# One core, a hybrid pooling and attention layer: its first stage (token scaling, q/k/v projections, q/k chains) with the weight bounds, the rotation, the transposes and the opening remade

## The chip, the cores and the metric

The kernel runs on one core of one Trainium2 chip. The metric is the device time of one execution in microseconds (us); the time before is the median of three runs. Smaller is better. The five engines are named as the profile names them: PE (TensorE), DVE (VectorE), ACT (ScalarE), POOL (GpSimd), SP (SyncE, which here only issues DMAs).

## What is computed

One layer over 2048 latent tokens and 256 context tokens of 1024 channels. The part that matters here is the front of it:

```python
h = _rmsnorm(x, norm_g) * (1.0 + scale[:, None, :]) + shift[:, None, :]
hc = _rmsnorm(xc, norm_g) * (1.0 + scale_c) + shift_c
p = _split_proj(h @ w_in)
...
def prep(t, nh, g):
    t = _rmsnorm(t.reshape(b, n, nh, -1), g)
    return t if tables is None else _rope_2d(t, tables)
...
def _rotate(x, cos, sin):
    m = x.shape[-1] // 2
    x1, x2 = x[..., :m], x[..., m:]
    return jnp.concatenate([x1 * cos - x2 * sin, x1 * sin + x2 * cos], axis=-1)
```

Each 64-wide head of q and k is normalised and rotated, its first 32 channels by the token's row in the grid and its last 32 by the column. Differential attention, grouped-query attention, pooling, gates and the two output projections follow. Scores are sums over the 64 channels, so an order of channels within a head that is the same for q and k changes nothing.

## The kernel before

All products run in split half precision: a float32 matrix is scaled by a power of two, written as a high and a low float16 part, and three products (high·high, high·low, low·high) are summed. The power of two comes from a bound on the largest absolute value.

There are three stages, one after the other. The first ends near 640 us, the second (attention, with gate columns computed between) and third (merge) take the rest; the diff does not touch those two.

The first stage, in order:

1. **Opening.** The two modulation vectors (`ada_product`, 16 weight blocks of 512 KB), then `modulation`, then `token_scale`, which bounds the modulated tokens over all partitions: a PE transpose to one row, a DVE maximum, and a PE product with a row of ones (`onerow`) that spreads it. `hfirst` and `hscaled` make the first 384 tokens (256 context, 128 latent) into float16 pairs. `w_prepare("dv")` bounds and splits the first weights.
2. **Five projections** in the order `QKV_ORDER` = dv, dk, dq, gq, gkv, called kinds below. The loop goes over tiles of 128 tokens: 18 tiles for dv, dk and gkv, 16 for dq and gq. `project` issues 24 products of 512 columns for a tile (256 columns for gkv) into one of three PSUM buffers `acc`, and then moves every open `qk_chain` one step.
3. **The q/k chain of a tile** is a generator with three steps, one step per later tile. Step one: squares on ACT (`sq`), their sums on DVE (`s`), and on POOL the power -1/2 (`r`, line 350) and the two products that join gain and rotation tables (`ab`). Step two: DVE normalises (`nt`), POOL multiplies by the cosine part (`rt`, line 362), DVE makes the sine part in two products (`m`, line 367), and DVE adds both (line 371). Step three: four PE transposes (`tpq`), ACT's high half and DVE's low half (`sp`, lines 378 and 379), stores by SP.
4. **Beside the products**, `beside` steps other generators in the middle of a tile: `w_prepare` of the next kind (line 436: a DVE maximum for each of 8 weight tiles; then `all_max`, a POOL reduction over partitions at line 420; then the split into halves, ACT and DVE), and `scan`, which reads the 40 gate columns (512 KB each) and takes a DVE maximum of each (line 471), and then `all_max` too. In gq, `ada_product` for the residual gate runs between the tiles.

Every engine executes its instructions in the order in which the code emits them, and SP issues DMAs in that order too, so an instruction that waits holds up all that stands behind it on its engine.

Of the kernel before, what the change touches and what calls it, by code (L numbers as in the profile page):

```python
# [35 lines left out]
HTOP = 8192.0  # L36
TINY = 2.0 ** -30
# [19 lines left out]
def block_kernel(ctx: ExitStack, tc, x, xT, ctxt, cc, ada_w, ada_bT, norm_gT, w_qkv, w_gate, gains,  # L57
# [149 lines left out]
    with tc.tile_pool(name="p1", bufs=1) as sp, tc.tile_pool(name="p1s", bufs=1, space=PSUM) as pp:  # L207
# [71 lines left out]
        def turned_tokens(g, k, gain, shift):  # L279

            nctx = max(0, min(3, NCT - 3 * g)) * P
            tp = tpx("tpx")
            for i in range(3):
                nc.tensor.transpose(out=tp[:, i * P:(i + 1) * P], in_=xs[g][i][:, k * P:(k + 1) * P], identity=ident)
            hf = sp.tile([P, GT], F32, name="hf", tag="hf", bufs=5)
            for a, b, m in ((0, nctx, 1), (nctx, GT, 0)):
                if b > a:
                    nc.scalar.activation(out=hf[:, a:b], in_=tp[:, a:b], func=AF.Identity, scale=gain[:, k, m:m + 1],
                                         bias=shift[:, k, m:m + 1])
            return hf  # L290

        def hfirst():

            for k in range(KT):
                hf0.append(turned_tokens(0, k, gainT, shiftT))
                yield

        def hscaled():
            for k in range(KT):
                hT[k] = s8("hT", [P, 2, SEQ], F16)  # L300
                for a, b, d in targets(0, k, 0):
                    nc.scalar.activation(out=d, in_=hf0[k][:, a:b], func=AF.Copy, scale=hsc[:, 0:1])
                for (a, b, d), (_, _, h) in zip(targets(0, k, 1), targets(0, k, 0)):
                    nc.vector.scalar_tensor_tensor(out=d, in0=hf0[k][:, a:b], scalar=hsc[:, 0:1], in1=h, op0=ALU.mult,
                                                   op1=ALU.subtract)
                yield
# [10 lines left out]
        def token_scale():  # L317
# [8 lines left out]
            row = tpx("hbt")  # L326
            nc.tensor.transpose(out=row[0:1, 0:P], in_=hb[:, 0:1], identity=ident)
            m1 = sp.tile([1, 1], F32, name="m1")
            nc.vector.tensor_reduce(out=m1, in_=row[0:1, 0:P], axis=AX.X, op=ALU.max)
            every = tpx("hbb")  # L330
            nc.tensor.matmul(every[:, 0:1], lhsT=onerow, rhs=m1, start=True, stop=True)
            nc.vector.tensor_scalar(out=hb[:, 1:2], in0=every[:, 0:1], scalar1=TINY, scalar2=None, op0=ALU.max)
# [6 lines left out]
        def qk_chain(ps, nh, gi, t, eps, dst):  # L339
# [11 lines left out]
            if t >= NCT:  # L351

                ab = sp.tile([P, 2, 64], F32, name="ab", tag="ab", bufs=3)
                nc.gpsimd.tensor_tensor(out=ab[:, :, 0:32], in0=rrow[:, t - NCT], in1=g4[:, gi, :, 0:32], op=ALU.mult)
                nc.gpsimd.tensor_tensor(out=ab[:, :, 32:64], in0=rcol, in1=g4[:, gi, :, 32:64], op=ALU.mult)
# [4 lines left out]
            rt = sp.tile([P, 512], F32, name="rt", tag="rt", bufs=2)  # L360
# [52 lines left out]
        def all_max(mx, name):  # L413

            m = sp.tile([P, 1], F32, name=name, tag="amx", bufs=2)
            nc.vector.tensor_reduce(out=m, in_=mx, axis=AX.X, op=ALU.max)
            nc.vector.tensor_scalar(out=m, in0=m, scalar1=TINY, scalar2=None, op0=ALU.max)
            r = sp.tile([P, 1], F32, name=name, tag="amr", bufs=2)
            from concourse import bass_isa
            nc.gpsimd.partition_all_reduce(out_ap=r, in_ap=m, channels=P, reduce_op=bass_isa.ReduceOp.max)  # L420
            return r
# [9 lines left out]
        def w_prepare(kind):  # L431

            width = QKV_CHUNKS[kind][1]
            mx = sp.tile([P, KT], F32, name="wmx", tag="wmx", bufs=2)
            for k in range(KT):
                nc.vector.tensor_reduce(out=mx[:, k:k + 1], in_=wraws[kind][k][:, :width], axis=AX.X, op=ALU.max,
                                        apply_absolute_value=True)
                yield
            r = all_max(mx, "wm")
            yield  # L440
            do, undo = scale_of(sp, HTOP, r, "ws")
            yield
            weights[kind] = []
            for k in range(KT):
                wr = wraws[kind][k]
                wt = sp.tile([P, 2, 512], F16, name="wt", tag="wt", bufs=16)
                nc.scalar.activation(out=wt[:, 0, :width], in_=wr[:, :width], func=AF.Copy, scale=do[:, 0:1])
# [14 lines left out]
        def scan():  # L462

            tiles = []
            for i in range(41):
# [4 lines left out]
                if i:  # L470
                    nc.vector.tensor_reduce(out=gmx[:, i - 1:i], in_=tiles[i - 1], axis=AX.X, op=ALU.max,
                                            apply_absolute_value=True)
                yield
            r = all_max(gmx, "gm")
            yield
            do, undo = scale_of(sp, HTOP, r, "gs")
# [9 lines left out]
        def project(kind, width, wt, t):  # L486
# [102 lines left out]
        for n, (half, k) in enumerate(blocks):  # L589
# [7 lines left out]
            if n == 8:  # L597
                modulation(0, ada_turn(rws))
            if n in (10, 11, 12, 13):
                next(hm)  # L600
        rws = ada_rows(aps[1])
        modulation(1, ada_turn(rws))
        hsc, hundo = token_scale()
        for _ in range(KT + 2):
            next(wp)
        hs = hscaled()
        for k in range(4):
            next(hs)
        for k in range(4):
            next(hm)  # L610
            next(hs)
            next(wp, None)
        for s in (hm, hs, wp):
            for _ in s:
                pass
        for _ in xnorm(1):
            pass
        scanning = scan()
        for n, kind in enumerate(QKV_ORDER):
# [12 lines left out]
            for t in range(first, NT):  # L632
# [8 lines left out]
                if n == 0:  # L641
# [8 lines left out]
                    if u >= 2:  # L650
                        at_step(coming, 4, *((7,) if u >= 12 else ()))
# [21 lines left out]
                if final:  # L673
                    if u < 2:
                        for _ in range(2):
                            next(scanning, None)
                    if u == 3:
                        for _ in scanning:
                            pass
                    if u in (4, 5):  # L680
                        col_load(u - 4)
                    if u == 9:
# [547 lines left out]
def make_inputs(i):  # L1230
# [13 lines left out]
    o["w_qkv"] = np.concatenate([sl(1536, 2048), sl(2048, 2560), sl(3584, 3840), sl(1024, 1536), sl(3072, 3584)], axis=1)  # L1244
# [3 lines left out]
    o["gains"] = np.stack([g, g.reshape(4, 2, 2, 16)[:, :, ::-1].reshape(4, 64)], axis=1)[None]  # L1248
# [43 lines left out]
```

## Time and profile before

| what | value |
|---|---|
| median of 3 runs | 3000.75 us (2998.82 to 3003.14) |
| the profiled execution's own time | 2999.54 us |
| its span | 2997.8 us |
| PE, DVE, ACT, POOL busy | 2800.9, 2322.5, 1569.1, 706.5 us |
| first stage: first qkv product to the end of gkv's | 54.8 to 632.9 us |

The span is the time from the first to the last profiled instruction; the time of the execution is 1.7 us longer. Busy times of different engines overlap. A row of a timeline gives start, length, engine, line, operation and tiles, and in brackets the idle time of the engine before the row and what ended it. A row of the table of stretches gives the stretch, its length, the busy time (and count) of the products of one line and of their weight loads, the granted clock, the DMA share and GB/s.

### The profile page before, as it was taken

To read this page: it belongs to the slowest core of one execution; us is meant where nothing else is said; L and a number is where in the kernel's file an instruction comes from. 1 tells how busy PE (TensorE), PEld (TensorE's weight loads), DVE (VectorE), ACT (ScalarE), POOL (GpSimd) and SP (SyncE) were. 2 spreads that over 40 slices of the span, in tenths; PEclk is the share of its full clock that TensorE was granted. 3 is DMA by queue.
4 is the path that set the end of the run, shared out by engine and by line. 5 is a ranking of instruction groups with operands and counts; after the bars stand their busy time and mean duration, and the time that the engine had idled before them with its cause. 6 is when DMAs were issued, how large, how long until landed. Compare 5 with 4: busy or idle time off the path is not lost. (4 is left out here: it accounts for less than half of the span.)

```text
span 2997.8 us, 40968 instructions
## 1 busy us (share of the span) xinstructions
PE 2800.9 (93%) x15013; PEld 1650.1 (55%) x15013; DVE 2322.5 (77%) x2953; ACT 1569.1 (52%) x2040; POOL 706.5 (24%) x689
## 2 busy tenths in 40 slices
PE   6997978889999999999999999999999997999999
PEld 1543433545555555555555556555565554787787
DVE  3557975649888889888889888889888875756753
ACT  3731111226766666666776777766777662223221
POOL 0024543540110111211112111111201114433431
PEclk8999989989999999999999999999999998999999
DMA  6233543238888888789899898899997986677674
GB/s 244 106 113 96 152 119 97 56 78 181 182 164 175 174 179 174 157 180 177 180 187 201 177 186 173 172 194 190 186 185 159 188 164 209 228 247 247 205 254 154
DMA packets 1134265, 516.45 MB, mean 172 GB/s; under 512 B 985040, under 2 KB 1038704, under 8 KB 1134064
## 3 DMA queue, kind: packets, MB, share of 16 engines
q1 hardware_dynamic: 1134064, 513.84, 72.9%
q8 instruction: 118, 1.93, 0.3%
q14 instruction: 83, 0.68, 0.1%
HBM read 208.24 MB, written 78.97 MB: 96 GB/s over the span
## 5 line engine op out<-in xcount | busy, mean ns | idle before, releaser
L177 PE MATMUL gate<-hT,gws 128*128 128x512 f16 x3840 | 871.7, 381 | 0.0
L177 PEld LDWEIGHTS <-gws 128*128 128x128 f16 x3840 | 374.1, 98 | 421.1 <-issue 21.0
L771 ACT ACTIVATE pt<-sa,nm,escale 128x1024 f32<-128x1024 f32 x256 | 308.3, 1204 | 451.9 <-DVE nm L768 400.8
L763 PEld LDWEIGHTS <-qt 128*128 128x128 f16 x2560 | 250.4, 98 | 354.4 <-issue 71.6
L491 PE MATMUL qkv<-wt,hT 128*128 128x512 f16 (+1 forms) x1920 | 399.8, 364 | 0.0
L767 DVE TENSOR_REDUCE nm<-sb 128x1 f32<-128x1280 f32 x256 | 379.1, 1481 | 0.5 <-PE sb L763 0.4
L766 DVE TENSOR_REDUCE nm<-sa 128x1 f32<-128x1024 f32 x256 | 311.2, 1216 | 72.1 <-PE sa L763 63.0
L772 ACT ACTIVATE pt<-sb,nm,escale 128x1280 f32<-128x1280 f32 x256 | 360.4, 1408 | 0.0
L854 DVE SCALAR_TENSOR_TENSOR lo<-pt,nm,hi 128x2304 f16<-128x2304 f32 x128 | 339.7, 2654 | 5.5 <-ACT hi L849 4.7
L763 PE MATMUL sb<-kt,qt 128*128 128x512 f16 (+1 forms) x1536 | 320.5, 345 | 18.5 <-ACT pt L772 17.5
L849 ACT ACTIVATE hi<-pt,nm 128x2304 f16<-128x2304 f32 x128 | 283.3, 2213 | 92.9 <-issue 49.3
L491 PEld LDWEIGHTS <-hT 128*128 128x128 f16 x1920 | 191.4, 100 | 182.6 <-issue 17.9
L763 PE MATMUL sa<-kt,qt 128*128 128x512 f16 x1024 | 263.4, 380 | 21.6 <-ACT pt L771 21.2
L1141 PE MATMUL br<-bt,wt 128*128 128x512 f32 x1152 | 268.7, 394 | 2.5 <-DVE wt L996 2.5
L894 PE MATMUL av<-th,vt 128*128 128x256 f16 x2304 | 262.6, 273 | 8.2 <-DMA th<-hi 5.4
L1141 PEld LDWEIGHTS br<-bt,wt 128*128 128x128 f32 x1152 | 217.7, 189 | 52.2 <-DVE wt L996 3.6
L894 PEld LDWEIGHTS <-vt 128*128 128x128 f16 x2304 | 225.1, 98 | 36.2 <-issue 6.0
L878 POOL TENSOR_TENSOR o<-ot 128x256 f32<-128x256 f32 x32 | 22.0, 687 | 841.5 <-ACT ot L874 799.4
L162 POOL TENSOR_SCALAR gws<-gw 128x512 f16<-128x512 f32 x74 | 75.6, 1022 | 604.1 <-PE gate L177 600.3
L378 ACT ACTIVATE sp<-tpq 128x512 f16<-128x512 f32 (+1 forms) x68 | 34.8, 512 | 318.0 <-PE tpq L376 315.4
L868 PE MATMUL av<-th,vt 128*128 128x256 f16 x1728 | 198.9, 273 | 0.0
L1173 PE MATMUL out<-y,wt 128*128 128x512 f32 x768 | 183.5, 397 | 12.0 <-DVE wt L996 5.3
(195 smaller groups left out, 3321.1 us busy)
## 6 DMA issues: line engine op xcount, KB each, us to landing
tD<-gt SPq DMA_DIRECT2D x96, 256.0 KB
wr<-in_w_br SPq DMA_DIRECT2D x32, 768.0 KB
ld<-tD SPq DMA_DIRECT2D x96, 256.0 KB
scan<-in_w_gate SPq DMA_DIRECT2D x40, 512.0 KB
gw<-in_w_gate SPq DMA_DIRECT2D x80, 256.0 KB
qt<-qD SPq DMA_DIRECT2D x256, 64.0 KB
wr<-in_w_out SPq DMA_DIRECT2D x32, 512.0 KB
sgD<-gt SPq DMA_DIRECT2D x48, 256.0 KB
```

What stands on the lines that cost most here:

```text
L177: nc.tensor.matmul(ps, lhsT=w[:, b, k, :], rhs=hT[k][:, a, c * CH:(c + 1) * CH], start=(n == 0), stop=(n == 3 * KT - 1))
L491: nc.tensor.matmul(ps[:, :width], lhsT=tokens_of(t, k, a), rhs=wt[k][:, b, :width], start=(n == 0), stop=(n == 3 * KT - 1))
L763: nc.tensor.matmul(dst, lhsT=qt[:, s, o * P:(o + 1) * P], rhs=kt[:, k0:k1], start=(s == 0), stop=(s == 1))
L766: nc.vector.tensor_reduce(out=nm[:, 0:1], in_=sa, axis=AX.X, op=ALU.max, negate=True)
L767: nc.vector.tensor_reduce(out=nm[:, 1:2], in_=sb, axis=AX.X, op=ALU.max, negate=True)
L771: nc.scalar.activation(out=pt[:, :SA], in_=sa, func=AF.Exp, scale=escale[:, m:m + 1], bias=nm[:, 0:1], accum_out=nm[:, 2:3])
L772: nc.scalar.activation(out=pt[:, SA:], in_=sb, func=AF.Exp, scale=escale[:, m:m + 1], bias=nm[:, 0:1], accum_out=nm[:, 3:4])
L849: nc.scalar.activation(out=box["hi"], in_=pt, func=AF.Copy, scale=nm[:, 3:4])
L854: nc.vector.scalar_tensor_tensor(out=lo, in0=pt, scalar=nm[:, 3:4], in1=box["hi"], op0=ALU.mult, op1=ALU.subtract)
L868: nc.tensor.matmul(ps[:, :256], lhsT=vt[:, k, v, :], rhs=pts[a][:, k, :], start=(n == 0), stop=(n == 3 * NKT - 1))
L894: nc.tensor.matmul(ps[:, :256], lhsT=vt[:, k, :, :].rearrange("p a d -> p (a d)"), rhs=pts[a][:, k, :], start=(n == 0), stop=(n == 2 * NKT ...
L1141: nc.tensor.matmul(ps, lhsT=wb[:, a, 4 * br + k, :], rhs=branch_tile(c, br, k)[:, b], start=(m == 0), stop=(m == 11))
```

## The change

- **Weight bounds.** The maximum over a weight tile on DVE becomes a sum of absolute values on ACT (`size_of`, scaled by 2^-24 and back; a sum is never below the maximum), for the weights of dk, dq, gq and gkv and for the 40 gate columns. The first weights (dv) keep the DVE maximum. The POOL reduction `all_max` is replaced by `over_partitions`, the PE way that `token_scale` used. The scale's top goes from 8192 to 16384 (`WTOP`).
- **Paired halves.** The channels of a head are reordered on the host, in weights and gains, so that both halves that a rotation swaps stand 32 apart. The sine part is then one DVE product of 512 instead of two of 256; POOL's two `ab` products go over 4 runs of 16 instead of 2 runs of 32.
- **Later transposes.** The addition leaves step two and becomes a step of its own, so a chain has four steps, and the transposes come one tile later. Chains move newest first. `rt` has three buffers instead of two, `m` two instead of one.
- **Opening.** dv's weights load before the last six modulation blocks; their maxima and the splits begin during the modulation products; POOL makes dv's high halves instead of ACT; half of the first tokens is scaled by a new `hsecond` straight from PSUM; the norms of the next 384 tokens (`xnorm(1)`) start earlier.

The diff, cut:

```diff
+        def hsecond():
+            for k in range(KT // 2, KT):
+                hT[k] = s8("hT", [P, 2, SEQ], F16)
+                tp = turned_raw(0, k)
+                hf = sp.tile([P, GT], F32, name="hf", tag="hf", bufs=4)
+                for (a, b, m), (_, _, d) in zip(spans(0), targets(0, k, 0)):
+                    nc.scalar.activation(out=d, in_=tp[:, a:b], func=AF.Identity, scale=gainS[:, k, m:m + 1],
+                                         bias=shiftS[:, k, m:m + 1])
+                    nc.vector.tensor_scalar(out=hf[:, a:b], in0=tp[:, a:b], scalar1=gainS[:, k, m:m + 1],
+                                            scalar2=shiftS[:, k, m:m + 1], op0=ALU.mult, op1=ALU.add)
+                for (a, b, d), (_, _, h) in zip(targets(0, k, 1), targets(0, k, 0)):
+                    nc.vector.tensor_tensor(out=d, in0=hf[:, a:b], in1=h, op=ALU.subtract)
+                yield
...
             if t >= NCT:
-                m2 = sp.tile([P, 512], F32, name="m2", tag="m2", bufs=1)
-                qv = lambda ap, a: hv(ap)[:, :, 32 * a:32 * a + 32].rearrange("p h (s j) -> p h s j", s=2)
-                for a in range(2):
-                    nc.vector.tensor_tensor(
-                        out=qv(m2, a), in0=qv(nt, a)[:, :, ::-1, :],
-                        in1=ab[:, 1:2, 32 * a:32 * a + 32].rearrange("p o (s j) -> p o s j", s=2).broadcast_to(
-                            [P, nh, 2, 16]), op=ALU.mult)
+                m2 = sp.tile([P, 512], F32, name="m2", tag="m2", bufs=2)
+                qv = lambda ap: hv(ap).rearrange("p h (s j) -> p h s j", s=2)
+                nc.vector.tensor_tensor(
+                    out=qv(m2), in0=qv(nt)[:, :, ::-1, :],
+                    in1=ab[:, 1:2].rearrange("p o (s j) -> p o s j", s=2).broadcast_to([P, nh, 2, 32]), op=ALU.mult)
+            yield
+            if t >= NCT:
                 nc.vector.tensor_tensor(out=rt[:, :W], in0=rt[:, :W], in1=m2[:, :W], op=ALU.add)
             yield
...
-        def all_max(mx, name):
...
-            nc.gpsimd.partition_all_reduce(out_ap=r, in_ap=m, channels=P, reduce_op=bass_isa.ReduceOp.max)
-            return r
+        def over_partitions(m, out):
+
+            row = tpx("row")
+            nc.tensor.transpose(out=row[0:1, 0:P], in_=m, identity=ident)
+            m1 = sp.tile([1, 1], F32, name="m1", tag="m1", bufs=2)
+            nc.vector.tensor_reduce(out=m1, in_=row[0:1, 0:P], axis=AX.X, op=ALU.max)
+            yield
+            every = tpx("every")
+            nc.tensor.matmul(every[:, 0:1], lhsT=onerow, rhs=m1, start=True, stop=True)
+            nc.vector.tensor_scalar(out=out, in0=every[:, 0:1], scalar1=TINY, scalar2=None, op0=ALU.max)
+
+        def size_of(dst, src):
+
+            junk = sp.tile([P, D], F16, name="junk", tag="xsq", bufs=1)
+            nc.scalar.activation(out=junk[:, :src.shape[-1]], in_=src, func=AF.Abs, scale=2.0 ** -24, accum_out=dst)
...
-            for c in list(chains):
+            for c in chains[::-1]:
                 if next(c, "end") == "end":
                     chains.remove(c)
...
-        for n in range(2, 16):
+        for n in range(2, 10):
             ada_load(n)
         for k in range(KT):
             w_load("dv", k)
+        for n in range(10, 16):
+            ada_load(n)
...
-            if n in (10, 11, 12, 13):
+            if n in (9, 10, 11, 12):
                 next(hm)
+            if n in (10, 11, 12, 13):
+                for _ in range(2):
+                    next(wp)
...
+        norming = xnorm(1)
+        for k in range(3):
+            next(norming)
         modulation(1, ada_turn(rws))
         hsc, hundo = token_scale()
```

What the emission order makes of it at two places, both on DVE. The first is one round in dk: one tile's worth of DVE instructions, from one normalisation (`nt`) to the next (`r` is POOL's power, `rt` POOL's cosine part, `m` DVE's sine part, `sp` the low half after the transposes). Before:

```order
L358 TENSOR_TENSOR nt<-qkv,r_1682 128x512
L367 TENSOR_TENSOR m_1732<-nt,ab 128x8x32 x2
L371 TENSOR_TENSOR rt<-rt,m_1732 128x512
L346 TENSOR_REDUCE s_1738<-sq 128x8
L347 TENSOR_SCALAR s_1738<-s_1738,wedk 128x8
L436 TENSOR_REDUCE wmx<-wraw 128x1
L471 TENSOR_REDUCE gmx<-scan 128x1
L379 TENSOR_TENSOR sp_1780<-tpq,sp_1780 128x512
L358 TENSOR_TENSOR nt<-qkv,r_1741 128x512
```

Of the change, the same place:

```order
L378 TENSOR_TENSOR nt<-qkv,r_1752 128x512
L386 TENSOR_TENSOR m_1792<-nt,ab 128x512
L391 TENSOR_TENSOR rt<-rt,m_1732 128x512
L399 TENSOR_TENSOR sp_1800<-tpq,sp_1800 128x512
L364 TENSOR_REDUCE s_1809<-sq 128x8
L365 TENSOR_SCALAR s_1809<-s_1809,wedk 128x8
L378 TENSOR_TENSOR nt<-qkv,r_1812 128x512
```

The two weight maxima are gone from between `s` and the next `nt`, `sp` stands ahead of `s`, and the addition is that of the tile before (`m_1732`, while the product just made is `m_1792`).

The second place is the opening, from the second `modulation` (the first row of before, `shiftT`) to the first low half of the tokens. Before:

```order
L242 TENSOR_TENSOR shiftT<-adat,abT 128x8
L243 TENSOR_TENSOR gainT<-adat,abT 128x8
...
L332 TENSOR_SCALAR hb<-hbb 128x1
L108 TENSOR_SCALAR hsu<-hb 128x1
L131 TENSOR_SCALAR hsu<-hsu 128x1
L132 RECIPROCAL hsd<-hsu 128x1
...
L436 TENSOR_REDUCE wmx<-wraw 128x1 x8
L416 TENSOR_REDUCE wm<-wmx 128x1
```

Of the change (`wsd` is the weights' scale, `hsd` the tokens'):

```order
L470 TENSOR_REDUCE wmx<-wraw 128x1 x8
L451 TENSOR_REDUCE wm<-wmx 128x1
...
L133 RECIPROCAL wsd<-wsu 128x1
L489 SCALAR_TENSOR_TENSOR wt<-wraw,wsd,wt 128x512 x4
L243 TENSOR_TENSOR shiftT<-adat,abT 128x8
L244 TENSOR_TENSOR gainT<-adat,abT 128x8
...
L133 RECIPROCAL hsd<-hsu 128x1
```

The eight maxima now stand ahead of the second modulation, and so do four low halves of the weights (`wt`), each of which needs a high half from POOL.

## Rows read from the trace of the kernel before

**Rows 1.** Stretches, products of line 491 alone: dk, dq, gq, gkv
```profile
182.55:308.30 125.75, 96.96 (x433) 42.59 (x432) 0.96 0.45 123
308.30:428.50 120.20, 88.23 (x384) 38.30 (x385) 0.93 0.45 122
428.50:563.80 135.30, 87.98 (x384) 37.65 (x385) 0.91 0.35 97
563.80:632.90 69.10, 54.29 (x432) 45.06 (x432) 0.93 0.25 65
```

**Rows 2.** Timeline of PE in dk: a tile's products and the transposes behind
```profile
198.58 5.34 PE L491 MATMUL qkv<-wt,hT 128*128 128x512 f16 x24
203.76 0.60 PE L376 MATMUL tpq<-ident,rt 128*128 128x128 f32 x4
204.19 2.11 PE L491 MATMUL qkv<-wt,hT 128*128 128x512 f16 x9
```

**Rows 3.** Timeline of DVE in dk, one round
```profile
231.65 0.68 DVE L358 TENSOR_TENSOR nt<-qkv,r 128x512 f32<-128x512 f32 x1
232.44 1.83 DVE L367 TENSOR_TENSOR m<-nt,ab 128x256 f32<-128x256 f32 x2
234.37 0.69 DVE L371 TENSOR_TENSOR rt<-rt,m 128x512 f32<-128x512 f32 x1
234.98 0.68 DVE L346 TENSOR_REDUCE s<-sq 128x8 f32<-128x512 f32 x1
235.70 0.23 DVE L347 TENSOR_SCALAR s<-s,wedk 128x8 f32<-128x8 f32 x1
...
237.56 0.68 DVE L379 TENSOR_TENSOR sp<-tpq,sp 128x512 f16<-128x512 f32 x1
238.16 0.68 DVE L358 TENSOR_TENSOR nt<-qkv,r 128x512 f32<-128x512 f32 x1
```

**Rows 4.** Timeline of POOL in dk, around the reduction over partitions
```profile
250.75 0.38 POOL L420 PARTITION_ALL_REDUCE wm<-wm  x1 [6.04 <-issue]
258.04 1.25 POOL L362 TENSOR_TENSOR rt<-nt,ab 128x512 f32<-128x512 f32 x1 [6.92 <-issue]
```

**Rows 5.** Timeline of the opening: PE, then DVE
```profile
70.54 4.05 PE L491 MATMUL qkv<-wt,hC 128*128 128x512 f16 x9
...
44.33 0.17 DVE L242 TENSOR_TENSOR shiftT<-adat,abT 128x8 f32<-128x8 f32 x1 [14.88 <-PE adat L232]
...
47.22 0.17 DVE L132 RECIPROCAL hsd<-hsu 128x1 f32<-128x1 f32 x1
```

**Rows 6.** Timeline of POOL in the round of rows 3
```profile
232.50 1.49 POOL L362 TENSOR_TENSOR rt<-nt,ab 128x512 f32<-128x512 f32 x1 [0.80 <-DVE nt L358]
236.01 1.64 POOL L350 TENSOR_TENSOR r<-s,mhalf 128x8 f32<-128x8 f32 x1 [2.02 <-DVE s L347]
237.61 0.32 POOL L354 TENSOR_TENSOR ab<-rrow,g 128x64 f32<-128x64 f32 x1
```

**Rows 7.** Timeline of DVE beside rows 4, while POOL does nothing else
```profile
245.11 0.76 DVE L367 TENSOR_TENSOR m<-nt,ab 128x256 f32<-128x256 f32 x2
```

**Rows 8.** Timeline of POOL in dk, beside two low halves of weights on DVE
```profile
274.54 2.07 POOL L350 TENSOR_TENSOR r<-s,mhalf 128x8 f32<-128x8 f32 x1 [2.02 <-DVE s L347]
```

**Rows 9.** Timeline of PE in gq: the residual gate's products, and two tiles' starts
```profile
444.07 3.53 PE L218 MATMUL ada<-aw,cct 128*2 128x512 f32 x4 [2.89 <-DMA aw<-in_ada_w]
...
455.07 5.35 PE L491 MATMUL qkv<-wt,hT 128*128 128x512 f16 x24
...
462.60 5.35 PE L491 MATMUL qkv<-wt,hT 128*128 128x512 f16 x24
```

**Rows 10.** Stretches, products of line 491 alone: the tile of dv with the reduction
```profile
143.30:149.30 6.00, 2.11 (x10) 0.78 (x8) 1.00 0.12 44
149.30:155.05 5.75, 4.98 (x15) 1.97 (x16) 0.70 0.01 1
```

**Rows 11.** Timeline of POOL in gkv: a scaling of 512 columns
```profile
606.01 0.69 POOL L158 TENSOR_SCALAR gw<-gw,gws 128x512 f32<-128x512 f32 x1
```

More of the change, by code (lines that the diff above doesn't have):

```diff
@@ L36 @@
 HTOP = 8192.0
+WTOP = 16384.0
 TINY = 2.0 ** -30
@@ L284, in turned_tokens @@
                 nc.tensor.transpose(out=tp[:, i * P:(i + 1) * P], in_=xs[g][i][:, k * P:(k + 1) * P], identity=ident)
[L285 to L289, printed above, removed]
+            return tp
+        def turned_tokens(g, k, gain, shift):
+            tp = turned_raw(g, k)
+            hf = sp.tile([P, GT], F32, name="hf", tag="hf", bufs=4)
+            for a, b, m in spans(g):
+                nc.scalar.activation(out=hf[:, a:b], in_=tp[:, a:b], func=AF.Identity, scale=gain[:, k, m:m + 1],
+                                     bias=shift[:, k, m:m + 1])
             return hf
         def hfirst():
-            for k in range(KT):
+            for k in range(KT // 2):
                 hf0.append(turned_tokens(0, k, gainT, shiftT))
@@ L298, in hscaled @@
         def hscaled():
-            for k in range(KT):
+            for k in range(KT // 2):
                 hT[k] = s8("hT", [P, 2, SEQ], F16)
@@ L325, in token_scale @@
                                            op0=ALU.mult, op1=ALU.add)
[L326 to L332, printed above, removed]
+            for _ in over_partitions(hb[:, 0:1], hb[:, 1:2]):
+                pass
             do, undo = scale_of(sp, HTOP, hb[:, 1:2], "hs")
@@ L353, in qk_chain @@
                 ab = sp.tile([P, 2, 64], F32, name="ab", tag="ab", bufs=3)
-                nc.gpsimd.tensor_tensor(out=ab[:, :, 0:32], in0=rrow[:, t - NCT], in1=g4[:, gi, :, 0:32], op=ALU.mult)
-                nc.gpsimd.tensor_tensor(out=ab[:, :, 32:64], in0=rcol, in1=g4[:, gi, :, 32:64], op=ALU.mult)
+                four = lambda ap: ap.rearrange("p a (s x j) -> p (a s) x j", s=2, x=2)
+                for axis, table in ((0, rrow[:, t - NCT]), (1, rcol)):
+                    nc.gpsimd.tensor_tensor(out=four(ab)[:, :, axis], in0=table.rearrange("p a (s j) -> p (a s) j", s=2),
+                                            in1=four(g4[:, gi])[:, :, axis], op=ALU.mult)
             yield
@@ L411, in value_scales, with largest @@
                                     op0=ALU.mult)
-        def all_max(mx, name):
[L415 to L419, printed above, removed]
-            nc.gpsimd.partition_all_reduce(out_ap=r, in_ap=m, channels=P, reduce_op=bass_isa.ReduceOp.max)
-            return r
+        def over_partitions(m, out):
[10 more added lines that the diff above has]
+            nc.scalar.activation(out=junk[:, :src.shape[-1]], in_=src, func=AF.Abs, scale=2.0 ** -24, accum_out=dst)
+        def largest(mx, name, scale=2.0 ** 24):
+            m = sp.tile([P, 2], F32, name=name, tag="amx", bufs=2)
+            nc.vector.tensor_reduce(out=m[:, 0:1], in_=mx, axis=AX.X, op=ALU.max)
+            nc.vector.tensor_scalar(out=m[:, 0:1], in0=m[:, 0:1], scalar1=scale, scalar2=None, op0=ALU.mult)
+            return m
         wraws, weights, wundo, weps = {}, {}, {}, {}
@@ L470, in scan @@
                 if i:
-                    nc.vector.tensor_reduce(out=gmx[:, i - 1:i], in_=tiles[i - 1], axis=AX.X, op=ALU.max,
-                                            apply_absolute_value=True)
+                    size_of(gmx[:, i - 1:i], tiles[i - 1])
                 yield
-            r = all_max(gmx, "gm")
+            m = largest(gmx, "gm")
             yield
-            do, undo = scale_of(sp, HTOP, r, "gs")
+            yield from over_partitions(m[:, 0:1], m[:, 1:2])
+            do, undo = scale_of(sp, WTOP, m[:, 1:2], "gs")
             nc.vector.tensor_scalar(out=gws, in0=do, scalar1=1.0, scalar2=None, op0=ALU.mult)
@@ L673, in block_kernel @@
                 if final:
[L674 to L679, printed above, removed]
+                    for _ in range(2 if u < 2 else 1):
+                        next(scanning, None)
                     if u in (4, 5):
                         col_load(u - 4)
-                    if u == 9:
+                    if u == 10:
                         col_split(0)
```

57 lines of the change are left out of this document (38 added, 19 removed).

## The prediction

> **What bounds the kernel now.** I read the profile stage by stage. The change touches the first stage only, so its worth is what TensorE loses there. First the table of stretches over one line's products [rows 1]: dk takes 125.75 us for 96.96 us of products, dq 120.20 for 88.23, gq 135.30 for 87.98, at granted clocks of 0.91 to 0.96. Then PE's timeline where nothing holds it back [rows 2]: 24 products take 203.76 - 198.58 = 5.18 us, and with four transposes one tile follows the next after 204.19 - 198.58 = 5.61 us. So dk's 18 tiles would need about 101 us and dq's 16 about 90. Two things take the rest.
>
> The first is DVE's round [rows 3]: from one `nt` to the next 238.16 - 231.65 = 6.51 us, with DVE busy almost throughout; TensorE's transposes wait for the addition at its end. The starts give its parts: `nt` to `m` 0.79, `m` to the addition 1.93, addition to `s` reduce 0.61, reduce to scaling 0.72, scaling to `sp` 1.86 (filled by the two weight maxima), `sp` to `nt` 0.60.
>
> The second is POOL's reduction over partitions [rows 4]. It takes 0.38 us itself, but POOL stands idle 6.04 us before it and 6.92 us after it, waiting for nothing that the profile shows, so `rt` comes 13 us late, the addition with it, and TensorE's clock falls as it idles. There are five of these beside the tiles: one each in dv, dk and dq (for the next kind's weights), two in gq (gate columns, gkv's weights).
>
> **The change, part by part.**
>
> *Reductions over partitions go to PE.* In its place stand one transpose, one DVE maximum of a row, one tiny product and four small DVE operations. Such a path exists already: from `shiftT` to `hsd` [rows 5] it took 47.22 - 44.33 = 2.89 us with the modulation arithmetic in front, so under 2.9 us. In the loop these steps lie between other tiles' work, on DVE in the time in which it waits for POOL's power, and I cost them at nothing; without that cover five times 2.9 us, 14 us. The Trainium skill ("GPSIMD Engine Reference", 4.1 Engine selection) speaks against this part: it recommends GpSimd for a reduction over the partition axis. By the rows the GpSimd way holds its engine 13 us and the PE way under 3; by the rule this part would win nothing, and the sum below would keep some 8 of its 61 us.
>
> *Weight maxima go to ACT.* They leave 1.86 us of the round, but only what is not waiting anyway is won. Between the scaling of `s` and the next `nt` stands POOL's power [rows 6]: 0.31 us to its start (236.01 - 235.70) and 1.64 us. Before, the maxima and `sp` covered it. After, DVE waits there with nothing to do. On ACT I estimate the sums at as much again (the same columns), some 1.9 us a tile; that lies beside the products, on an engine that was busy for 1569.1 of 2997.8 us and has two other operations in a round. Cost nothing; without that cover, the 1.9 us would stand in the round in place of the wait for POOL, which is as long.
>
> *One sine product instead of two.* This is where the round is decided. The pair of products took 0.76 us when POOL did nothing beside it [rows 7], and 1.83 us when POOL's `rt` ran [rows 3]: `rt` started 0.06 us after the first product and ended at 233.99 [rows 6], and the second product ended 0.28 us later, at 234.27. So the second waited for the whole of `rt`. After the change the single product starts first and passes, but the next instruction is the addition, which also reads two tiles; and POOL's `rt` is by then ahead of it. I reckon that the wait moves from the second product to the addition. The Trainium skill ("SBUF — State Buffer", Who interferes with whom) has the rule: DVE with two SBUF inputs and a GpSimd operation that reads SBUF share one port, and whichever starts first blocks the other throughout. The rows agree for a product that reads what `rt` reads (0.76 against 1.83); by the rule the addition, which reads other tiles, is held as well, which no row shows.
>
> The new round, from starts: `nt` to `m` 0.79. 256 columns more cost some 0.27 us (the second product, of 256, took 0.28 once `rt` had ended), so `rt` ends 1.55 + 0.27 = 1.82 us after `m` starts; the addition ends 0.28 + 0.27 = 0.55 after that, and what follows starts 0.08 before (234.37 + 0.69 against 234.98): 2.29. `sp` to the reduce 0.60, to the scaling 0.72, to the power 0.31, the power 1.64, then `nt`. Sum 6.35 us. In four tiles of a kind two low halves of weights delay the power to 2.07 us [rows 8], 0.43 more. If the addition is not held, it takes 0.61 instead of 1.69 and the round is 5.27 us, under PE's 5.61: then PE sets the pace. These are the bounds; I take 6.35, since the rows show exactly this pair of engines blocking.
>
> *Transposes a step later.* This gives PE slack at a kind's start, not a shorter round: DVE loses 0.74 us a tile (6.35 - 5.61) and PE waits once the slack is gone. I let half of dk (9 tiles, 3 of them without transposes) run at PE's pace; bounds 2 and 18 tiles, 6 us either way.
>
> *dk:* 3 x 5.18 + 6 x 5.61 + 9 x 6.35 + 4 x 0.43 = 108.1, from 125.8: -17.7.
> *dq:* 16 x 6.35 + 1.7 = 103.3, from 120.2: -16.9.
> *gq:* the gate's products set tiles 2 to 8: 462.60 - 455.07 = 7.53 us each [rows 9], on PE itself, so DVE catches up. The second tile waited 2.89 us for a load and ran its products at low clock (3.53 us). That load stands on SP behind the stores of `sp`, which now come a tile later, so I put this tile at 16 us instead of 5.61 + 2.89 + 3.53 = 12 (bounds 12 and 19). 6.35 + 16 + 7 x 7.53 + 5 x 5.61 + 2 x 6.35 + 1 = 116.8, from 135.3: -18.5.
> *gkv:* half the columns, small operations, no reduction over partitions within it, POOL's gate-column split still in it: unchanged at 69.1; bounds -10 and +5.
> *dv:* PE sets its pace, but for one tile with a reduction in it [rows 10]: 6.00 us with 2.11 us of products, then 5.75 us at a clock of 0.70. 3.9 and 0.3 x 5.75 = 1.7 go: -5.6.
>
> *Opening.* The maxima move under the modulation products, where DVE idled 14.88 us [rows 5]. But the scale now stands before the second modulation, and four low halves behind it, each waiting for a high half that POOL makes in about 0.69 us [rows 11] while it blocks DVE on the port, as above. That is 0.69 and then four times 1.3 (0.69 for POOL, 0.6 for DVE, in turn), 5.9 us: the second modulation comes near 50 us instead of 44.33, `hsd` near 53 instead of 47.22. Behind it the eight maxima (8 x 0.6 us) are gone and half the weight halves are done, but `hsecond` adds two DVE operations for each of four slices, and POOL's other four high halves alternate with DVE again. I get `xt` normalised and PE resumed at 68.5 us instead of 70.54: -2. Bounds: -10 (no blocking) and +4.
>
> Sum: 2 + 5.6 + 17.7 + 16.9 + 18.5 = 61 us. Against the profiled execution, 2999.5 - 61 = 2938.5 us (that execution stands 1.2 us under the median). The later stages keep their instructions, and I keep their time. The rounds save 0.16 us in each of some 40, about 6 us, and with the opening some 8; the five reductions are the rest.
>
> **Rivals.**
> - *PE sets the pace:* the addition slips past POOL. dk 3 x 5.18 + 15 x 5.61 = 99.7, dq 89.8, gq 5.6 + 12 + 52.7 + 7 x 5.61 = 109.6; with -7.6 ahead -90, so 2910. For it: the addition reads other tiles than `rt` does. Against: the wait is `rt`'s whole length, as of an engine that is shut out, not of two that share a tile.
> - *Less than forecast:* the PE path's small steps are not covered (+14), the opening loses 4 us and gkv 5: -61 + 14 + 6 + 5 = -36, 2963.5.
> - *Slower:* the reshaped `ab` products. Each takes 0.32 us [rows 6], the pair ends before `m` starts. If runs of 16 make POOL slower, the pair holds `m` and `rt`: the round grows by all beyond 0.8 us. With 40 rounds at DVE's pace, 61 us are gone when the pair takes 2.3 us; at 2.8 us the kernel takes about 3020. Against: 64 elements, and only their runs change.
>
> **How the numbers follow.** Forecast (2928 to 2950) 0.66, PE pace 0.15, less than forecast 0.14, slower 0.03, neither 0.02. 2938.5 is the forecast's; 2905 to 2965 takes in the two nearer rivals. 0.2% (6 us) is about what a measurement tells from no change: faster 0.95, within it 0.02, slower 0.03.
>
> **What would show it.** Right: an addition of about 1.7 us in dk, ending just after POOL's `rt`; DVE idle some 1.7 us before `nt`, ended by POOL's `r`; tiles 6.3 us apart late in dk and dq; no gap of 6 us on POOL between dv's start and gkv's. Wrong: an addition of 0.69 us and tiles 5.6 us apart (PE pace); PE waiting for `m1` or `every`; the first product later than 57 us, or dv's second tile later than 80; a clock under 0.9 in dk or dq.

## The result and the profile after

The changed kernel takes 2946.32 us (median of 4 runs, 2944.99 to 2947.69) against 3000.41 us (2998.82 to 3003.14) beside it on the same chip: a ratio of 0.9819, interval 0.9802 to 0.9836, so 54 us faster. 2938.5 was forecast. The profiled execution has a span of 2945.9 us against 2997.8; the first stage ends at 581.22 us, 51.65 us earlier than before, so the whole gain lies in the stage that was changed.

The stretches of dk, dq, gq and gkv after the change (columns as in [rows 1]; the products now stand on line 532):

```profile
177.05:284.29 107.24, 95.97 (x434) 42.20 (x433) 1.00 0.50 138
284.29:391.10 106.81, 87.44 (x384) 37.89 (x384) 0.98 0.51 138
391.10:510.17 119.07, 86.72 (x384) 36.88 (x384) 0.97 0.42 111
510.17:581.22 71.05, 54.55 (x432) 45.00 (x431) 0.90 0.27 69
```

dk became 18.5 us shorter, dq 13.4 and gq 16.2; gkv became 2 us longer. The granted clock in dk is 1.00, where it was 0.96: the stall around the reduction, in which it fell, is gone. One round of VectorE in dk, to be laid beside [rows 3]:

```profile
221.46 0.69 DVE L378 TENSOR_TENSOR nt<-qkv,r 128x512 f32<-128x512 f32 x1 [1.75 <-POOL r L368]
222.25 0.69 DVE L386 TENSOR_TENSOR m<-nt,ab 128x512 f32<-128x512 f32 x1
222.86 1.75 DVE L391 TENSOR_TENSOR rt<-rt,m 128x512 f32<-128x512 f32 x1
224.54 0.68 DVE L399 TENSOR_TENSOR sp<-tpq,sp 128x512 f16<-128x512 f32 x1
225.14 0.67 DVE L364 TENSOR_REDUCE s<-sq 128x8 f32<-128x512 f32 x1
225.85 0.23 DVE L365 TENSOR_SCALAR s<-s,wedk 128x8 f32<-128x8 f32 x1
227.82 0.69 DVE L378 TENSOR_TENSOR nt<-qkv,r 128x512 f32<-128x512 f32 x1 [1.75 <-POOL r L368]
```

and POOL in the same round, beside [rows 6]:

```profile
222.32 1.75 POOL L382 TENSOR_TENSOR rt<-nt,ab 128x512 f32<-128x512 f32 x1 [0.33 <-DVE nt L378]
226.16 1.64 POOL L368 TENSOR_TENSOR r<-s,mhalf 128x8 f32<-128x8 f32 x1 [2.09 <-DVE s L365]
```

The round is 227.82 - 221.46 = 6.36 us, against 6.51. The sine product passes in 0.69 us, and the addition behind it takes 1.75 us and ends (224.61) 0.54 us after GpSimd's `rt` (224.07). In front of `nt` VectorE stands idle 1.75 us until GpSimd's power has run. So 1.75 - 0.69 + 1.75 = 2.8 us of the round are waits for GpSimd.

The opening (PE, then DVE), beside [rows 5]:

```profile
69.04 1.04 PE L288 MATMUL tpx<-ident,xt 128*128 128x128 f32 x2 [7.30 <-DVE xt L268]
...
70.54 4.02 PE L532 MATMUL qkv<-wt,hC 128*128 128x512 f16 x9
...
49.50 0.15 DVE L243 TENSOR_TENSOR shiftT<-adat,abT 128x8 f32<-128x8 f32 x1
...
52.69 0.17 DVE L133 RECIPROCAL hsd<-hsu 128x1 f32<-128x1 f32 x1
```

TensorE resumes at the same 70.54 us. And two waits for loads that were shorter before: in dq for a gate column, now on ScalarE (before on VectorE, at most 1.2 us), and TensorE's in gq (beside [rows 9], where it was 2.89 us):

```profile
296.62 0.19 ACT L447 ACTIVATION_READ_ACCUMULATOR junk<-wraw 128x1 f32 x1
304.63 1.06 ACT L447 ACTIVATE junk<-scan 128x1024 f16<-128x1024 f32 x1 [7.83 <-DMA scan<-in_w_gate]
...
305.69 0.58 ACT L398 ACTIVATE sp<-tpq 128x512 f16<-128x512 f32 x1
...
411.00 3.57 PE L219 MATMUL ada<-aw,cct 128*2 128x512 f32 x4 [6.56 <-DMA aw<-in_ada_w]
```

### The profile page after: what moved, and what is told of

The parts are those of the page before. It is cut to its first block, busy times and chain, and to the rows that moved or that the text cites. A ratio compares the mean times of both kernels' runs of the same rounds, so it can differ in the third digit from the quotient of the medians.

```text
span 2945.9 us, 41046 instructions
## 1 busy us (share of the span) xinstructions
PE 2792.9 (95%) x15031; PEld 1651.4 (56%) x15031; DVE 2268.9 (77%) x2837; ACT 1623.4 (55%) x2168; POOL 723.1 (25%) x691
## 3 DMA queue, kind: packets, MB, share of 16 engines
q8 instruction: 118, 1.93, 0.3%
## 5 line engine op out<-in xcount | busy, mean ns | idle before, releaser
L811 PE MATMUL sb<-kt,qt 128*128 128x512 f16 (+1 forms) x1536 | 320.6, 345 | 18.5 <-ACT pt L820 17.5
L942 PEld LDWEIGHTS <-vt 128*128 128x128 f16 x2304 | 225.3, 98 | 36.3 <-issue 5.1
L916 PEld LDWEIGHTS <-vt 128*128 128x128 f16 x1728 | 169.1, 98 | 19.7
```

The costliest lines, as they stand in the source:

```text
L811: nc.tensor.matmul(dst, lhsT=qt[:, s, o * P:(o + 1) * P], rhs=kt[:, k0:k1], start=(s == 0), stop=(s == 1))
L916: nc.tensor.matmul(ps[:, :256], lhsT=vt[:, k, v, :], rhs=pts[a][:, k, :], start=(n == 0), stop=(n == 3 * NKT - 1))
L942: nc.tensor.matmul(ps[:, :256], lhsT=vt[:, k, :, :].rearrange("p a d -> p (a d)"), rhs=pts[a][:, k, :], start=(n == 0), stop=(n == 2 * NKT ...
```

## The experiments

Theory, from the prediction: (a) most of the gain is the five reductions over partitions that leave GpSimd; (b) the round barely shortens, since the addition is shut out while GpSimd's `rt` runs, and VectorE waits uncovered for GpSimd's power. Rivals: the gain is the lighter VectorE (maxima, one product) or the later transposes; or the addition waits for something else than the port. Each ratio stands against the kernel before on the same chip (2998.67, 3001.18 and 3000.33 us in the three groups), so a difference of 2 us between edits of different groups says little. The later stages, which no edit touches, took 2364 to 2370 us in the profiled executions; where that matters, the end of the first stage is given beside the time.

**Reductions alone.** The kernel before, with `all_max` replaced (the five beside the tiles, and the one for dv's weights in the opening), and nothing else:

```diff
-            r = all_max(mx, "wm")
+            m = largest(mx, "wm")
             yield
-            do, undo = scale_of(sp, HTOP, r, "ws")
+            yield from over_partitions(m[:, 0:1], m[:, 1:2])
+            do, undo = scale_of(sp, HTOP, m[:, 1:2], "ws")
```

> The kernel before with one part of the change alone: the five reductions over partitions go through TensorE (a transpose, a row maximum, a product by ones). Theory (these five are most of the gain): the tiles of 15 to 20 us in dk, dq and gq go, VectorE's round stays at 6.5 us, and the time falls by 42 to 52 us, to 2948 to 2958. Rival (the gain comes from the shorter load of VectorE, the merged product and the later transposes): under 20 us, 2980 or more.

2949.27 us, ratio 0.9834 (0.9818 to 0.9851). Its stretches of dk, dq, gq and gkv:

```profile
179.77:293.30 113.53, 96.14 (x434) 42.23 (x433) 1.00 0.51 136
293.30:399.26 105.96, 87.02 (x385) 37.85 (x384) 0.98 0.52 139
399.26:513.79 114.53, 86.14 (x384) 36.77 (x384) 0.99 0.41 115
513.79:581.69 67.90, 51.30 (x432) 43.54 (x431) 0.97 0.25 67
```

49 of the 54 us, with a round still of 6.50 us; the intervals of this kernel and of the whole change overlap. The first stage ends at 581.69 us here and at 581.22 after the whole change, so the other three parts together won 0.5 us of it: what they win ahead of dk (2.7 us) and in dk (6.3) they give back in dq (0.9), gq (4.5) and gkv (3.2). Most of the 3 us between the two times lies behind the first stage.

**Reductions put back.** The changed kernel, with `partition_all_reduce` in `over_partitions`' place for the weights and the gate columns:

```diff
-            yield from over_partitions(m[:, 0:1], m[:, 1:2])
+            yield from pool_max(m)
```

> The changed kernel with the five reductions over partitions put back on GpSimd, all else as changed. Theory: GpSimd stands idle some 6 us before each reduction and 7 us after, so 38 to 52 us come back: 2984 to 2998. Rival (with the later transposes and a shorter VectorE load the slack covers GpSimd's 13 us): under 20 us come back, 2966 or less.

2987.90 us, ratio 0.9964 (0.9951 to 0.9977): 41.6 us come back. POOL in dk:

```profile
246.00 0.38 POOL L448 PARTITION_ALL_REDUCE wm<-wm  x1 [5.97 <-issue]
254.37 1.25 POOL L382 TENSOR_TENSOR rt<-nt,ab 128x512 f32<-128x512 f32 x1 [8.00 <-issue]
```

The two idle times of [rows 4] again, and a tile of 18.97 us in dk. The slack from the later transposes does not cover them there, in dq or in gq; in dv, where no work for GpSimd stands close behind the reduction now, no tile is longer. The first stage ends at 615.91 us, 34.7 later than with the change; most of the rest of the 41.6 lies behind it, and no edit explains it.

**Maxima back on VectorE.** `size_of` in the changed kernel is VectorE's maximum again:

```diff
-            nc.scalar.activation(out=junk[:, :src.shape[-1]], in_=src, func=AF.Abs, scale=2.0 ** -24, accum_out=dst)
+            nc.vector.tensor_reduce(out=dst, in_=src, axis=AX.X, op=ALU.max, apply_absolute_value=True)
```

> The changed kernel with the maxima of weights and gate columns put back from ScalarE onto VectorE (maxima instead of sums). Theory (VectorE waits for GpSimd's power in that place anyway): the round stays within 0.15 us of 6.37, and the time within 6 us of the changed kernel's: 2940 to 2952. Rival (taking 1.3 us of maxima off VectorE is what shortened the round): the round grows to 7.5 us and the time by 30 us or more.

2952.19 us (0.9842; 0.9828 to 0.9857), 6 us above the change; the intervals overlap, and the first stage ends 4.8 us later. The round stays at 6.37 us, 6.97 beside the weight splits (6.80 after the change). dq's stall grows, to tiles of 12.20 and 7.71 us, with VectorE waiting 5.46 us for a load of the scan: the stall belongs to the load, not to ScalarE.

**One product alone.** The kernel before with the paired halves side by side and the single sine product:

```diff
-                for a in range(2):
-                    nc.vector.tensor_tensor(
-                        out=qv(m2, a), in0=qv(nt, a)[:, :, ::-1, :],
-...
+                nc.vector.tensor_tensor(
+                    out=qv(m2), in0=qv(nt)[:, :, ::-1, :],
```

> The kernel before with one part of the change alone: paired halves side by side and one sine product instead of two, the addition still in the same step. Theory (VectorE waits out GpSimd's product there, now ahead of the addition, which needs that product, instead of inside the second sine product): the round shortens by only 0.2 to 0.35 us, from 6.51 to 6.2 to 6.3, and the time falls by 5 to 12 us, to 2988 to 2995; the five reductions still cost what they did. Rival (a product of 0.7 us less in each round): 0.7 us or more a round, 25 us or more.

2998.95 us, ratio 0.9990 (0.9981 to 1.0000): no gain that shows, less than I expected, though the profiled execution's first stage ends 4.9 us earlier. The round is 6.42 us, only 0.09 shorter. DVE, then POOL:

```profile
238.53 0.69 DVE L368 TENSOR_TENSOR m<-nt,ab 128x512 f32<-128x512 f32 x1
240.38 0.69 DVE L371 TENSOR_TENSOR rt<-rt,m 128x512 f32<-128x512 f32 x1 [1.16 <-POOL rt L364]
...
238.60 1.75 POOL L364 TENSOR_TENSOR rt<-nt,ab 128x512 f32<-128x512 f32 x1 [0.80 <-DVE nt L360]
```

The product takes 0.69 us instead of a pair of 1.83, and the addition starts 1.85 us after it instead of 1.93: `rt`, held by a longer first product, takes 1.75 us instead of 1.49, and VectorE waits for it.

**The port.** The changed kernel, with the sine product of dk and dq written to PSUM; order, sizes and semaphores stay:

```diff
-                m2 = sp.tile([P, 512], F32, name="m2", tag="m2", bufs=2)
+                m2 = tpx("m2") if nh == 8 and gi < 2 else sp.tile([P, 512], F32, name="m2", tag="m2", bufs=2)
```

> The changed kernel with the sine product of dk and dq written to PSUM, so that the addition has one operand from SBUF and one from PSUM; order and sizes unchanged. Theory (the addition is shut out because it and GpSimd's product both read SBUF by two operands through one port): the addition takes about 0.7 us though GpSimd's product still runs, the round falls under 5.62 us, dk and dq run at TensorE's pace, and the time falls by 15 to 25 us, to 2921 to 2931. Rival (the addition waits for GpSimd's product through a semaphore or a shared tile): it still ends just behind that product, and the time stays at 2943 to 2949.

2921.94 us, ratio 0.9737 (0.9722 to 0.9751). DVE and POOL in a round of dq, then the stretches of dk and dq:

```profile
323.77 0.70 DVE L386 TENSOR_TENSOR m<-nt,ab 128x512 f32<-128x512 f32 x1
324.38 0.68 DVE L391 TENSOR_TENSOR rt<-rt,m 128x512 f32<-128x512 f32 x1
...
323.83 1.75 POOL L382 TENSOR_TENSOR rt<-nt,ab 128x512 f32<-128x512 f32 x1 [0.34 <-DVE nt L378]
...
177.08:277.39 100.31, 95.97 (x433) 42.17 (x432) 1.00 0.57 151
277.39:367.78 90.39, 85.77 (x384) 37.51 (x384) 1.00 0.61 162
```

The addition runs in 0.68 us in the midst of GpSimd's product, and dk and dq run at TensorE's pace. What shuts the addition out is that it takes two operands from SBUF; no semaphore or shared tile does.

**Order of the chains.** In the changed kernel the newest chain is served first. Served oldest first, the difference and the addition stand ahead of `nt` and `m`:

```diff
-            for c in chains[::-1]:
+            for c in list(chains):
```

> The changed kernel with the chains served oldest first, so that on VectorE the difference of t-3 and the addition of t-2 stand ahead of the rescaling and the sine product of t-1. Theory (the addition is held because it meets GpSimd's product of the next tile; moved ahead of that product it lies in the wait for GpSimd's power): the addition takes about 0.7 us instead of 1.75, VectorE's round falls from 6.37 us to under 5, TensorE sets the pace of 5.62 us through dk and dq, and the time falls by 20 to 28 us, to 2918 to 2926. Rival (VectorE's round is full for other reasons, or the addition is slow wherever it stands): rounds stay at 6.3 us or more and the time at 2943 to 2950.

2903.36 us, ratio 0.9680 (0.9666 to 0.9695): 43 us less than the change, more than I expected. DVE, POOL, and the stretches:

```profile
244.42 0.68 DVE L391 TENSOR_TENSOR rt<-rt,m 128x512 f32<-128x512 f32 x1
245.02 0.68 DVE L378 TENSOR_TENSOR nt<-qkv,r 128x512 f32<-128x512 f32 x1
245.81 0.69 DVE L386 TENSOR_TENSOR m<-nt,ab 128x512 f32<-128x512 f32 x1
246.42 0.68 DVE L364 TENSOR_REDUCE s<-sq 128x8 f32<-128x512 f32 x1
247.13 0.52 DVE L365 TENSOR_SCALAR s<-s,wedk 128x8 f32<-128x8 f32 x1
...
245.87 1.75 POOL L382 TENSOR_TENSOR rt<-nt,ab 128x512 f32<-128x512 f32 x1 [1.96 <-DVE nt L378]
...
176.37:276.68 100.31, 95.97 (x433) 42.21 (x432) 1.00 0.56 151
276.68:367.91 91.23, 85.79 (x385) 37.38 (x385) 1.00 0.61 162
367.91:479.84 111.93, 86.63 (x384) 36.88 (x384) 0.98 0.43 117
479.84:538.74 58.90, 51.49 (x432) 43.01 (x431) 0.94 0.32 81
```

The addition and the difference now stand between the scaling of `s` and the next `nt`, where VectorE waited for GpSimd's power, and `rt` does not run there. What stands beside `rt` is a reduction with one operand, which it does not hold (0.68 us). The round is TensorE's 5.62 us; in this place VectorE now waits 1.77 us for ScalarE's high half, which waits for TensorE's transposes. dk to gkv take 41.8 us less than after the change. I had not counted gkv, which runs most of its tiles at TensorE's 2.73 us instead of 3.42, nor gq's second tile (12.73 us instead of 16.61).

**Chain as before.** Oldest first and also the addition back in the step of the sine product, which undoes the later transposes:

```diff
-            for c in chains[::-1]:
+            for c in list(chains):
...
-            yield
             if t >= NCT:
                 nc.vector.tensor_tensor(out=rt[:, :W], in0=rt[:, :W], in1=m2[:, :W], op=ALU.add)
```

> The changed kernel with the steps of the q/k chain and their order as before: the addition in the same step as the sine product, older chains first; so the transposes stand one step earlier. Theory (VectorE's round is then 2.64 us from the rescaling to the addition, 0.61, 0.72, 0.31 and 1.64, as the kernel before with one product shows where no maxima stand in it: 5.95 us): dk and dq lose 7 to 15 us against the changed kernel, and the time is 2908 to 2928. Rival (the later transposes are part of the gain): VectorE's round at 6.4 us or more, the time 2944 or more.

2937.39 us, ratio 0.9789 (0.9774 to 0.9803): between the two expectations. The round is 5.95 us, as worked out, but 6.38 beside the weight splits, dq keeps a stall (tiles of 8.02 and 7.30 us) and gkv takes 68.6 us. Some 5 us more than after the change lie behind the first stage, which no step here explains. So by the times the later step, served newest first, costs 9 us against the chain of before, and served oldest first it is worth 34; by the ends of the first stage (565.00 us here, 581.22 and 538.74) it is 16 and 26.

**Opening.** Two edits of the changed kernel, each alone: dv's four early low halves behind the token scale, and the second group's normalisations earlier:

```diff
         next(wp)
-        for _ in range(2):
-            next(wp)
         norming = xnorm(1)
```

> The changed kernel with dv's first four low halves of weights moved behind the token scale. Theory (these halves and GpSimd's high halves take VectorE in turn and hold the second modulation): the token scale's reciprocal comes near 48 us instead of 52.5 and the first normalised tile some 2 to 3 us earlier, so 2941 to 2945. Rival (VectorE's total work up to the normalised tiles decides, in whatever order): the reciprocal comes earlier, but dv's second tile still starts at 75.5 to 77 us, and the time is within 2 us of the changed kernel's 2946.

```diff
             next(h2)
+            if k == 0:
+                for _ in norming:
+                    pass
             next(wp, None)
```

> The changed kernel with the three normalisations of the second group of tokens put behind the first of the four slices of the second half instead of behind all. Theory (TensorE's queue stands at the transposes of the second group, which wait for these, while the products behind them could run): dv's second tile starts at 71 to 73.5 us instead of 76.35, and the time falls by 3 to 5 us, to 2941 to 2943. Rival (the last slices and weight halves end the first tile anyway, and come 2.2 us later): the start is at 75.5 to 78 us and the time within 2 us of 2946.

The first: 2945.60 us (0.9819; 0.9804 to 0.9833), no difference that shows. `hsd` comes at 47.77 us instead of 52.69 and dv's second tile at 74.56 instead of 76.35, nearer the rival. The second: 2942.62 us (0.9808; 0.9793 to 0.9823), with dv's second tile at 71.70. The intervals overlap with that of the change; the tile's start, 4.65 us earlier, is in the trace.

**Weight loads spread.** The next kind's eight loads two ahead of each of four tiles:

```diff
-            if not final:
-                for k in range(KT):
-                    w_load(QKV_ORDER[n + 1], k)
...
+                if not final and u < KT // 2:
+                    for k in (2 * u, 2 * u + 1):
+                        w_load(QKV_ORDER[n + 1], k)
```

> The changed kernel with the eight weight loads of the next kind issued two ahead of each of the kind's first four tiles, instead of all ahead of the first. Theory (in dq's fourth tile ScalarE waits for a scan load queued behind those eight, with the copies and squares of the chains behind it): the stall of 9.98 and 7.29 us there goes or shrinks to under 2 us, and the time falls by 3 to 5.5 us, to 2941 to 2943. Rival (another load or the stores hold the scan load): the stall stays and the time is within 2 us of 2946.

2943.50 us (0.9810; 0.9795 to 0.9824): the interval overlaps with that of the change, but dq's stretch is 3.6 us shorter and has no tile above 6.81 us:

```profile
285.32:388.56 103.24, 85.77 (x384) 37.49 (x384) 1.00 0.55 143
```

**A version that beats both.** First the three edits (oldest first, normalisations earlier, loads spread) together, then two more: gq's loads for the gate's modulation are issued ahead of `project`, and the first gate column is split like the weights, by ScalarE and VectorE:

```diff
+                if n == 0:
+                    nc.scalar.activation(out=hi, in_=wr, func=AF.Copy, scale=gws[:, 0:1])
+                    nc.vector.scalar_tensor_tensor(out=lo, in0=wr, scalar=gws[:, 0:1], in1=hi, op0=ALU.mult,
+                                                   op1=ALU.subtract)
+                    continue
```

> The changed kernel with three edits together: oldest chains first, the second group's normalisations earlier, the next kind's weight loads spread. If they add up, from 2903.4: the opening's 4 us, and 0.8 us for what is left of dq's stall: 2897 to 2900. Rival (the spread loads or the earlier start collide with something else): 2902 to 2906.

> The three edits, and two more: the loads for the gate's modulation are issued ahead of the tile's projections instead of behind them, and the first gate column is split by ScalarE and VectorE instead of GpSimd. Theory: gq's second tile falls from 12.7 us to about 7.6 us, and gkv's two tiles of 7.4 and 4.8 us to 2.7 to 3.5 us each, so 8 to 12 us less than the three edits alone: 2886 to 2891. Rival (the loads wait for their buffers, or the split holds VectorE as long): under 3 us less.

Three edits: 2895.52 us, ratio 0.9650 (0.9636 to 0.9665), so they add up and a little more. Five: 2889.55 us, 0.9632 (0.9615 to 0.9648), that is 57 us below the change. The stretches with five:

```profile
172.03:272.34 100.31, 95.97 (x434) 42.14 (x432) 1.00 0.57 151
272.34:362.73 90.39, 85.78 (x385) 37.47 (x385) 1.00 0.62 163
362.73:468.96 106.23, 86.15 (x385) 36.73 (x385) 1.00 0.46 124
468.96:521.05 52.09, 49.49 (x432) 41.78 (x431) 1.00 0.36 89
```

dk and dq are at the 101 and 90 us that the prediction read off [rows 2] for TensorE's pace, and no stretch loses clock. Against three edits the two more give 6 us by the times, not 8 to 12, and 8.6 us by the ends of the first stage: gkv's two tiles of 7.40 and 5.14 us take 2.76 and 2.73, while gq's second tile was at 8.98 us with three edits already, and is at 7.52 now.

## Why the prediction was right, and where it was not

The mechanism was right: the reductions made the gain, and in the round the wait moved to the addition. The sum was 9 us too large against the first stage (61 predicted, 51.65 measured); the misses lie in dq (3.5 us), gq (2.3), gkv (2.0), the opening (1.5) and dv (0.5), and dk came out 0.8 us better.

- *Reductions.* Predicted as all but some 8 of the 61 us, so 53; measured 49 alone, and 42 put back (51.2 and 34.7 in the first stage). The other reading that the prediction named, that this part wins nothing, is refuted. That the small steps cost nothing holds nearly: where TensorE sets the pace their transpose and product stand in its queue and make two tiles 0.1 and 0.4 us longer, 0.5 us for each reduction. These are the two instructions in dk with the oldest chains first, in tiles of 5.72 and 6.03 us where the others take 5.62:

```profile
233.82 0.27 PE L436 MATMUL row<-ident,wm 128*1 128x128 f32 x1
...
239.64 0.38 PE L441 MATMUL every<-m,onerow 1*128 1x1 f32 x2
```

- *Round.* 6.35 predicted, 6.36 measured; 6.78 beside weight splits predicted, 6.80 measured. The wait did move from the second product to the addition, and a wait for GpSimd's power did open where the maxima had been. The rule of the Trainium skill ("SBUF — State Buffer", Who interferes with whom) that two SBUF operands on VectorE and a GpSimd operation that reads SBUF shut each other out was the doubtful link; the addition's 1.75 us beside `rt` against 0.68 with one operand in PSUM agrees with it. That the first blocks the other throughout does not hold for GpSimd's power: two low halves of weights, which read two operands from SBUF, run beside it in the 1.41 us that they also take with GpSimd idle (57.20 in the kernel before), and the power takes 2.07 us instead of 1.64. DVE, then POOL, in dk after the change, and DVE in the opening before:

```profile
265.07 1.41 DVE L489 SCALAR_TENSOR_TENSOR wt<-wraw,wsd,wt 128x512 f16<-128x512 f32 x2
...
265.24 2.07 POOL L368 TENSOR_TENSOR r<-s,mhalf 128x8 f32<-128x8 f32 x1 [2.09 <-DVE s L365]
...
57.20 1.41 DVE L448 SCALAR_TENSOR_TENSOR wt<-wraw,wsd,wt 128x512 f16<-128x512 f32 x2
```

- *Transposes later.* Half of dk at TensorE's pace was a choice, and that it came so near is luck; ten of 18 tiles were. dk came out at 107.2 us for 108.1.
- *dv.* 5.6 us predicted, 5.1 measured: the tile of 11.76 us takes 6.58, of which the two instructions above are the part that was not counted.
- *dq.* 103.3 predicted, 106.8 measured. The step "16 x 6.35 + 1.7" has no term for the scan load that queues behind the eight weight loads. Before, it made tiles of 8.01 and 7.09 us; after, of 9.98 and 7.29. With the loads spread the same stretch took 103.24 us. The wait now stands on ScalarE, which "cost nothing" had counted by its busy time alone, but the growth is not due to ScalarE: with the sums there and the chain as before the tiles are 8.02 and 7.30 us, and with the maxima on VectorE in the changed kernel 12.20 and 7.71. With the addition freed by PSUM, and the loads as they were, no tile of dq is above 6.03 us. So the wait costs a tile what the chains leave it no slack for; what of the chain's order makes it grow is not shown.
- *gq.* 116.8 predicted, 119.1 measured. The late load was foreseen (16 us, measured 16.61), and so was its reason: with the chain as before, whose stores come a tile earlier, that tile takes 12.51 us. The third tile at 8.12 and the last two at 6.54 were not foreseen.
- *gkv.* Predicted unchanged, measured 2 us longer. One chain more of gq is outstanding: the transposes of three of its tiles stand among gkv's products where two did. The first three tiles take 6.53, 6.78 and 5.45 us where they took 6.03, 6.03 and 2.73; the third ran its products at a granted clock of 0.55, almost all at the lower of the two levels, in 5.18 us instead of 2.78, after TensorE had stood idle for 3.28 and 3.12 us. Two later tiles take 2 us less together. The diff also spreads the scan's last steps over more tiles and moves the split of the first gate column one tile on, which no run tests alone.
- *Opening.* 2 us predicted, 0.5 measured (dv's second tile from 76.83 to 76.35). The times of the second modulation (50 us, measured 49.50) and of `hsd` (53, measured 52.69) were right; that fewer maxima behind `hsd` bring the normalised tiles earlier was wrong: TensorE resumed at 70.54 us as before, not at 68.5. One sign of being wrong did come: the first product starts at 58.54 us, later than the 57 that the prediction named (54.81 before). dv's second tile was not late for it. Moving the halves away bought 1.8 us of the tile's start, moving the normalisations 4.65: TensorE's queue stands at the second group's transposes while its next products could run.

The rival "PE sets the pace" gave dk 99.7 and dq 89.8 us; with the addition freed they took 100.31 and 90.39, the small steps included. It failed only at the condition it named. "Slower" did not occur: the `ab` pair keeps its 0.32 us each.

## What to carry to other kernels

Before counting an instruction as saved, ask which wait stands behind it: here two products made one, and maxima moved off, left a round that GpSimd set, and only the reductions paid. Where two engines shut each other out, move the work within the order, or one operand to PSUM, rather than shorten it: one line of order was worth 43 us, four fifths of the change. An operation that reads a load brings the load's wait in front of everything queued behind it, on whichever engine it stands, and the wait costs as much as the chains have no slack for.

## What the hardware showed that I had not expected

- The shutting-out works both ways: GpSimd's `rt` takes 1.75 us beside VectorE's sine product, and 1.25 us where none stands beside it (reductions put back, 254.37).
- It holds small operations too: VectorE's scaling of 128x8 takes 0.52 us beside `rt` and 0.23 otherwise, while a reduction of 128x512 with one operand keeps its 0.68.
- GpSimd's way back from the reduction to ordinary operations costs more than the way there: 8.00 us against 5.97 with the reductions put back, and 6.92 to 8.00 against 5.83 to 6.07 at four reductions of the kernel before, all with nothing to wait for that the profile shows.
